# Block 1 of a three-block network: the delta rule and the gated branch written in turns of small steps

## The chip, the cores and the metric

One core of a Trainium2 chip runs the whole kernel as a single program. The metric is device time in microseconds (us), as the median of several runs. Engines are named as in the profile: PE is TensorE's matmuls and PEld its weight loads, DVE is VectorE, ACT is ScalarE, POOL is GpSimd, and SP is SyncE, which issues nearly all DMAs.

## The reference, cut to what matters

The reference has a first block and then a second one of depth two. Only the first block is touched. It works on 512 latent and 256 context positions of width 1024. From one normalized input and one projection it feeds three branches, whose results stand side by side, are multiplied by a gate and projected back:

```python
y_rc, y_rl = _rwkv_branch(u_c, u_l, ...)      # delta rule: 6 heads of 64, 2 directions
o_hc, o_hl = _hgrn_branch(fh_c, fh_l, ...)    # gated branch: 6 heads of 64, 2 directions
pool_l = _pool_branch(pv_l, True, pool_w[l], pool_scale[l])
mix_l = jnp.concatenate([pool_l, y_rl, o_hl], axis=-1) * jax.nn.silu(g_l)
new_x = _layer_norm(ALPHA * h_x + gt_l[:, None] * (mix_l @ w_out[l])) * ln_g[l] + ln_b[l]
```

The delta rule updates a matrix of 64x64 for each head and position, `S = S * w - (S kk) (kk a)^T + v k^T`, and reads it with `r`. The gated branch updates `S = exp(log f) * S + k i^T` and reads it with `q`. Both run over the context first and then, from that state, over the latent positions, once forwards and once backwards. They do not depend on each other.

## The kernel before

Both branches take two heads at a time, as 128 partitions, so there are three pairs `p`.

**The delta rule** is the generator `rwkv_pair(p)`. Its preparation makes the projections, the low-rank decay and rate (their bias is L690), and `rwkv_prep`, which builds the keys `BK` and the queries `AR` for both directions. Then come three groups `g` (context, and two halves of the latent positions), each of four chunks of 64 positions, with both directions side by side. A group has a state-free part, `rwkv_pre`: the score products (L763), transposes, and the inverse of a triangular matrix for each chunk, on VectorE and TensorE in turns. Its four calls of `rwkv_chunk` pass the state `st` on: POOL scales it (`pe`, L922), TensorE multiplies, ScalarE copies (`xs`), TensorE multiplies by the inverse, ScalarE and VectorE write `uv`, TensorE multiplies, and VectorE writes the new state (`rS`, L945, once for each direction). Then `rwkv_out` reads the group and `gate` projects one block of the output gate. The last group is followed by the pair's `readout` (its last line is L665). It yields after the preparation and after the first and second group.

**The gated branch** is `hgrn_pair(p)`: the projections `q` and `i`, and for each direction `dd` the projection `z` and one `hgrn_unit`. I number these six units 0 to 5 (pair 0 has units 0 and 1). A unit prepares the cumulated logarithms `hg` (first line L1048) and keys `kd`, then passes six chunks of 128 positions: two of the context, which only update the state `hS` (L1130), and four latent ones, for which `hgrn_levels` builds seven levels of products and each head's scores are reduced (`hrd`, L1096), copied to `sct` by ScalarE and multiplied. Its pair ends with a normalization (L1011). It yields once for each unit. Its projections write the PSUM tile `mf`, those of the delta rule `mm`; both go through `dense` (L277), which splits each weight block into two parts on ScalarE (L263) and VectorE (L264).

**Order.** `block1` draws steps of both generators in a loop over `n`:

```python
next(rw)
for n in range(6):
    for _ in range(2 - n % 2):
        next(rw, None)
    next(hg)
    ...                      # modulation: self.ada(...), and for n == 0 the pool branch
```

So an even `n` writes two groups of the delta rule and then a unit; an odd `n` writes the third group, the readout and the next pair's preparation, and then a unit. Behind each follows a modulation product (`ada`, matmuls L318 on weights that SP loads). The order in which a program is written is a rank for the library that lays out each engine's queue: an instruction whose inputs are ready goes by rank, and one that ranks later may stand ahead of one that is not ready. Each engine then works its queue in order, and waits for other engines through semaphores that the library places. Most tiles have one buffer, so that a unit's `z` or `hg` is not written before the unit ahead has read it. Behind the loop, `gated` multiplies the branches by the gate, and the next stage normalizes the context and projects with `w_out`.

Of the kernel before, what the change touches and what calls it, by code (L numbers as in the profile page):

```python
# [197 lines left out]
class B:  # L198
# [228 lines left out]
    def block1(self):  # L427
# [20 lines left out]
        with ExitStack() as ctx:  # L448
            ctx.enter_context(self.banks(mm=2, rsc=2, rch=1, mf=2, ma=1))
            ctx.enter_context(self.stream("f", 2, 1))  # L450
            ctx.enter_context(self.stream("a", 3, 1))
            self.scr = ctx.enter_context(tc.tile_pool(name="scr", bufs=1, space=bass.MemoryType.DRAM))
            self.f1 = ctx.enter_context(tc.tile_pool(name="f1", bufs=1))
            self.f2 = ctx.enter_context(tc.tile_pool(name="f2", bufs=2))
            self.con1 = self.f1.tile([128, CONST.shape[1] - NCON], F32, name="con1")
            nc.sync.dma_start(self.con1, d["const"][:, NCON:])
            self.ymix = self.scr.tile([128, 8, NL], F32, name="ymix")
            self.ygate = self.scr.tile([128, 8, NL], F32, name="ygate")
            self.ar = [[self.f1.tile([128, 4, 2, 2 if g else 1, 64], F32, name=f"AR{g}{dd}") for dd in range(2)] for g in range(3)]
            self.tt = self.f1.tile([128, 8, 2, 64], F32, name="rtt")  # L460
            for a in (*chain(*self.ar), self.tt):
                nc.gpsimd.memset(a, 0.0)
            self.sct = [self.f1.tile([128, 2, 128], F32, name=f"sct{a}") for a in range(2)]
            for x in self.sct:
                nc.gpsimd.memset(x, 0.0)
            self.rwkv_lora()
            self.hgrn_lb()
            self.last = {}
            rw = chain.from_iterable(self.rwkv_pair(p) for p in range(3))
            hg = chain.from_iterable(self.hgrn_pair(p) for p in range(3))  # L470
            next(rw)
            for n in range(6):
                for _ in range(2 - n % 2):
                    next(rw, None)
                next(hg)
                if n == 0:
                    self.ada(s, 0, d["mod_w"], 1, 2, mod[:, 16:24], self.V("mod_b", 16, 8), "a")
                    self.pool_branch()
                l, g = divmod(n, 3)
                self.ada(s, 2, d["ada_w"][l], g, 4, self.m2[l][:, 16 * g:16 * g + 16],  # L480
                         self.V("ada_b_2", 48 * l + 16 * g, 16), "a")
            hh, hl = self.htiles()

            def gated(j, y=None):
                a = y or self.f1.tile([128, NL], F32, tag=("tw", "ta")[j % 2], name="ga")
                b = self.f1.tile([128, NL], F32, tag=("G", "km")[j % 2], name="gb")
                if y is None:
                    nc.sync.dma_start(a, self.ymix[:, j])
                nc.sync.dma_start(b, self.ygate[:, j])
                nc.gpsimd.tensor_tensor(b, a, b, op=ALU.mult)  # L490
                self.split(hh[:, j, 256:], hl[:, j, 256:], b)

            for j in (0, 1, 2, 3, 5, 6):
                gated(j)
            for _ in chain(rw, hg):
                pass
            for j in (4, 7):
                gated(j, self.last[j])
# [116 lines left out]
    def rwkv_pair(self, p):  # L615
# [25 lines left out]
        for g in range(3):  # L641
            pre = self.rwkv_pre(g, bk, v)
            sts = []
            for i in range(4):
                sts.append(st)
                st = self.rwkv_chunk(g, i, ec[:, :, 4 * g + i], pre, st)
            if g:
                self.rwkv_out(g, sts, pre, y)
            if 3 * p + g < 8:
                self.gate(3 * p + g)  # L650
            if g < 2:
                yield
# [330 lines left out]
    def hgrn_pair(self, p):  # L983
        nc = self.nc
        f1, f2 = self.f1, self.f2
        q = f1.tile([128, NL], F32, name="hq")
        o, = self.dense(self.d["w_in"], 13 + p, self.hh, self.hl, (LAT,), st="f")
        nc.scalar.copy(q, o)
        it = f1.tile([128, 6, 128], F32, name="hit")
        ft = f1.tile([128, NT], F32, tag="htmp", name="hif")  # L990
        for (c0, cn), o in zip((LAT, CTX), self.dense(self.d["w_in"], 16 + p, self.hh, self.hl, (LAT, CTX), st="f")):
            nc.scalar.copy(ft[:, c0:c0 + cn], o[:, :cn])
        for c0, n in ((2, 4), (0, 2)):
            tp = self.psum("mf", (128, 4, 128))
            for j in range(n):
                nc.tensor.transpose(tp[:, j], ft[:, (c0 + j) * 128:(c0 + j + 1) * 128], self.C("ident"))
            nc.scalar.copy(it[:, c0:c0 + n], tp[:, :n])
        oa = f1.tile([128, NL], F32, name="hoa")
        for dd in range(2):
            z = f1.tile([128, NT], F32, name="hz")  # L1000
            for (c0, cn), o in zip((LAT, CTX), self.dense(self.d["w_in"], 19 + 3 * dd + p, self.hh, self.hl, (LAT, CTX), st="f")):
                nc.scalar.copy(z[:, c0:c0 + cn], o[:, :cn])
            self.hgrn_unit(p, dd, q, it, z, oa)
            yield
        sq = f1.tile([128, NT], F32, tag="htmp", name="osq")
        nc.gpsimd.tensor_tensor(sq[:, :NL], oa, oa, op=ALU.mult)
        va = self.psum("mf")
        nc.tensor.matmul(va, self.C("bones"), sq[:, :NL], start=True, stop=True)
        rs = f1.tile([128, NT], F32, tag="hg", name="ors")
        self.rsqrt_bc(rs[:, :NL], [(rs[:, :NL], va)], 1.0 / 64, 1)  # L1010
        nc.vector.scalar_tensor_tensor(oa, oa, self.V("hgrn_norm_g", p), rs[:, :NL], op0=ALU.mult, op1=ALU.mult)  # L1011
        self.last[5 + p] = oa
        if p < 2:
            nc.sync.dma_start(self.ymix[:, 5 + p], oa)
# [27 lines left out]
    def hgrn_unit(self, p, dd, q, it, z, oa):  # L1042
# [19 lines left out]
        for c in range(6):  # L1062
            nc.scalar.activation(kd[:, c], g[:, c], AF.Exp, scale=-1.0, bias=g[:, c, end:end + 1])
        nc.vector.tensor_tensor(kd, kd, k, op=ALU.mult)
        s = f2.tile([128, 128], F32, name="hS")
        nc.gpsimd.memset(s, 0.0)
        order = (0, 1, 2, 3, 4, 5) if dd == 0 else (1, 0, 5, 4, 3, 2)
        for n, c in enumerate(order):
# [49 lines left out]
            if n < 5:  # L1118
# [9 lines left out]
                for h in range(2):  # L1128
                    H = slice(64 * h, 64 * h + 64)
                    nc.vector.scalar_tensor_tensor(s2[H, H], s[H, H], ge[H, c:c + 1], tp[H, 1, 0:64], op0=ALU.mult, op1=ALU.add)  # L1130
                s = s2


    def block2(self):
# [646 lines left out]
```

## Time and profile before

| | us |
|---|---|
| median of 3 runs | 2727.29 (2724.37 to 2738.44) |
| profiled execution | 2736.78 |
| its span, first to last instruction | 2735.0 |
| PE busy in the span | 2523.7 (92%) |
| DVE / ACT / POOL busy | 1621.3 / 1276.9 / 319.3 |
| block 1's two branches | about 90 to 850 of the span |

The profile is one execution. "Busy" of PE counts matmuls that overlap and whose ends are modelled. PEclk is the clock granted to TensorE, as a share of 2.4 GHz; it has two levels, 1.0 and 0.5, so that a value between is a mean over a stretch. A row of a source line gives how often its instruction ran in a stretch, its duration, and when the first and the last of them started.

### The profile page before, as it was taken

The page shows a single profiled execution, that of the slowest core. Times are in us where ns is not written, and L with a number is a line of the kernel's source. Part 1 is how long each engine was busy: PE and PEld are TensorE (multiplying, and loading weights), DVE is VectorE, ACT ScalarE, POOL GpSimd, SP SyncE. Part 2 cuts the span into 40 slices and gives each one's busy share as a digit, 9 for nine tenths or more (in the row PEclk, how much of TensorE's full clock was granted, in tenths as well). Part 3 has the DMA queues.
Part 4 walks back from the last instruction along what each step waited for, and adds up shares of the span by engine and source line. Part 5 has one row for each costly group of instructions (what it writes and reads, how often), then busy time and mean ns, then how long its engine had stood idle before and what let it go on. Part 6 is the DMA issues. An engine that isn't in the chain of part 4 may idle for free.

```text
span 2735.0 us, 53289 instructions
## 1 busy us (share of the span) xinstructions
PE 2523.7 (92%) x21320; PEld 1990.5 (73%) x21320; DVE 1621.3 (59%) x3815; ACT 1276.9 (47%) x2840; POOL 319.3 (12%) x432
## 2 busy tenths in 40 slices
PE   7989979979877989989899999999998999999998
PEld 3655646545546777777677888888886888888888
DVE  4566574576565656777856443344463767664665
ACT  3454454545455656556434332233344555542444
POOL 0121121122112000111110110011000000010010
PEclk9999989989887999999989999999998999999999
DMA  6233432434334211111231112212231102233325
GB/s 206 77 94 118 139 98 92 125 100 134 93 104 146 72 39 32 36 41 37 65 105 47 62 63 64 63 63 66 80 105 44 32 27 95 78 100 93 100 89 157
DMA packets 159016, 231.10 MB, mean 84 GB/s; under 512 B 12976, under 2 KB 90032, under 8 KB 158768
## 3 DMA queue, kind: packets, MB, share of 16 engines
q1 hardware_dynamic: 158768, 227.70, 26.7%
q8 instruction: 167, 2.74, 0.4%
q14 instruction: 81, 0.66, 0.1%
HBM read 217.95 MB, written 9.70 MB: 83 GB/s over the span
## 4 chain that ended last, share of the span: by engine, by line
PE 47%; DVE 2%; ACT 2%; issue 1%; POOL 1%; DMA 0%; POOLq 0%; SPq 0%; DVEq 0%; ACTq 0%
PE mm L277 39%; PE ms L1735 2%; PE mt L1754 1%; PE mv L351 1%; PE mt L1748 1%; PE mm L1685 1%; PE mf L277 0%; DVE hl L423 0%; DVE ht L421 0%; POOL qr L1669 0%; ACT hh L422 0%; DMA raw<-mla_w_out 0%; ACT whi L263 0%; ACT qrh L1705 0%; PE mm L1665 0%
## 5 line engine op out<-in xcount | busy, mean ns | idle before, releaser
L264 DVE TENSOR_TENSOR wlo<-raw,whi 128x512 fp32r<-128x512 f32 (+3 forms) x560 | 391.3, 701 | 395.1 <-ACT whi L263 236.6
L263 ACT CAST whi<-raw 128x512 fp32r<-128x512 f32 (+3 forms) x560 | 331.9, 594 | 462.8 <-PE mm L277 398.9
L277 PE MATMUL mm<-hh,whi 128*128 128x512 f32 (+1 forms) x1960 | 483.8, 360 | 28.0 <-ACT hh L422 13.6
L277 PE MATMUL mm<-hl,whi 128*128 128x512 f32 (+1 forms) x1960 | 457.3, 350 | 0.0
L277 PE MATMUL mm<-hh,wlo 128*128 128x512 f32 (+1 forms) x1960 | 455.3, 350 | 0.4 <-DVE wlo L264 0.4
L277 PEld LDWEIGHTS mm<-hh,whi 128*128 128x128 f32 x1960 | 332.4, 192 | 89.7 <-ACT hh L422 21.0
L277 PEld LDWEIGHTS mm<-hl,whi 128*128 128x128 f32 x1960 | 329.7, 193 | 46.8 <-issue 3.6
L277 PEld LDWEIGHTS mm<-hh,wlo 128*128 128x128 f32 x1960 | 328.9, 193 | 45.0 <-issue 2.0
L1233 POOL TENSOR_TENSOR fc<-fc,fc 128x768 f32<-128x768 f32 (+1 forms) x44 | 69.2, 1573 | 867.9 <-DVE fc L585 625.8
L277 PE MATMUL mm<-fh,whi 128*128 128x256 f32 (+1 forms) x616 | 136.3, 340 | 1.0 <-ACT fh L398 1.0
L583 DVE SCALAR_TENSOR_TENSOR fc<-mm,vec,fc 128x511 f32<-128x511 f32 (+1 forms) x132 | 86.8, 658 | 80.7 <-ACT fc L582 80.7
L277 PE MATMUL mm<-fl,whi 128*128 128x256 f32 (+1 forms) x616 | 130.5, 330 | 0.0
L277 PE MATMUL mm<-fh,wlo 128*128 128x256 f32 (+1 forms) x616 | 129.3, 328 | 0.0
L582 ACT ACTIVATE fc<-mm,vec 128x512 f32<-128x512 f32 (+1 forms) x132 | 81.4, 617 | 97.2 <-PE mm L277 97.2
L277 PEld LDWEIGHTS mm<-fh,whi 128*128 128x128 f32 x616 | 99.8, 190 | 15.8 <-issue 3.4
L318 PE MATMUL ma<-raw,cvs 128*32 128x256 f32 x832 | 95.6, 427 | 15.3 <-DMA raw<-ada_w 10.6
L277 PE MATMUL mf<-hh,whi 128*128 128x512 f32 (+1 forms) x360 | 103.6, 387 | 6.0 <-ACT whi L263 3.4
L277 PEld LDWEIGHTS mm<-fl,whi 128*128 128x128 f32 x616 | 99.0, 190 | 11.3 <-issue 0.5
L1197 DVE SCALAR_TENSOR_TENSOR xr<-mm,m,xr 128x512 f32<-128x512 f32 (+1 forms) x112 | 66.5, 597 | 67.0 <-PE mm L277 66.8
L277 PEld LDWEIGHTS mm<-fh,wlo 128*128 128x128 f32 x616 | 98.6, 190 | 10.4
L351 PE MATMUL mv<-sq,con 128*128 128x256 f32 (+1 forms) x240 | 84.3, 452 | 12.4 <-ACT sq L355 12.0
L277 PE MATMUL mf<-hl,whi 128*128 128x512 f32 (+1 forms) x360 | 95.4, 367 | 0.0
(545 smaller groups left out, 4383.6 us busy)
## 6 DMA issues: line engine op xcount, KB each, us to landing
raw<-ada_w SPq DMA_DIRECT2D x96, 512.0 KB, 4.6
raw<-ffn_up SPq DMA_DIRECT2D x176, 256.0 KB, 2.8
raw<-ffn_down SPq DMA_DIRECT2D x96, 256.0 KB, 2.7
raw<-w_in SPq DMA_DIRECT2D x66, 256.0 KB, 2.9
raw<-ab_w_in SPq DMA_DIRECT2D x50, 256.0 KB, 2.6
raw<-ffn_down SPq DMA_DIRECT2D x48, 192.0 KB, 2.4
raw<-mod_w SPq DMA_DIRECT2D x16, 512.0 KB, 7.6
raw<-w_out SPq DMA_DIRECT2D x32, 256.0 KB, 2.9
```

Source lines behind the costliest of these rows:

```text
L263: nc.scalar.copy(hi[:, :nk], raw[:, :nk])
L264: nc.vector.tensor_tensor(lo[:, :nk], raw[:, :nk], hi[:, :nk].bitcast(F32), op=ALU.subtract)
L277: nc.tensor.matmul(o, a[:, k], b[:, k0 + k, t:e], start=(k0 == 0 and j == 0 and k == 0), stop=(k0 + n == nk and j == 2 and k == n - 1))
L318: nc.tensor.matmul(acc[32 * b:32 * b + 32, c:c + 256], s[:, k, :], t[:, b], start=(k == 0), stop=(k == 7))
L351: self.nc.tensor.matmul(v[:, :x.shape[1]], self.C("ones"), x, start=(k == 0), stop=(k == 7))
L582: nc.scalar.activation(out[:, c0:c0 + cn], o[:, :cn], AF.Copy, scale=w[1])
L583: nc.vector.scalar_tensor_tensor(out[:, c0 + 1:c0 + cn], o[:, :cn - 1], w[0], out[:, c0 + 1:c0 + cn], op0=ALU.mult, op1=ALU.add)
L1197: nc.vector.scalar_tensor_tensor(x, o[:, :cn], gcol(m, 0 if c0 else 1), x, op0=ALU.mult, op1=ALU.add)
L1233: nc.gpsimd.tensor_tensor(g, g, u, op=ALU.mult)
L1685: nc.tensor.matmul(o[:, e], a[:, k, T], b[:, k], start=(i == 0), stop=(i == 5))
L1735: nc.tensor.matmul(o[:, at:at + cn], a, b, start=(j == 0), stop=(j == 4))
L1748: nc.tensor.transpose(tp[:, j], p[:, (c0 + j) * 128:(c0 + j + 1) * 128], self.C("ident"))
```

## The change

No instruction is added or left out. Both generators get more places to yield, and the loop takes turns between them.

```diff
             next(rw)
             for n in range(6):
-                for _ in range(2 - n % 2):
-                    next(rw, None)
-                next(hg)
+                for i in range(4):
+                    next(hg)
+                    for _ in range(1 + (i == 1 and n % 2 == 0)):
+                        next(rw, None)
...
             for i in range(4):
+                if i % 2 == 0:
+                    yield
                 sts.append(st)
                 st = self.rwkv_chunk(g, i, ec[:, :, 4 * g + i], pre, st)
...
-            self.hgrn_unit(p, dd, q, it, z, oa)
+            yield from self.hgrn_unit(p, dd, q, it, z, oa)
             yield
...
         nc.vector.tensor_tensor(kd, kd, k, op=ALU.mult)
+        yield
         s = f2.tile([128, 128], F32, name="hS")
...
                 s = s2
+            if n in (1, 3):
+                yield
```

A step of the delta rule is now a state-free part, or the first two chunks of a group, or its last two with what follows them (output, gate, and after the third group the readout and the next preparation): nine steps for each pair. A step of the gated branch is the projections and the preparation of a unit, or its two context chunks, or two latent chunks with their levels: four steps for each unit. In each turn the gated step is written first. An even `n` writes: unit's preparation, state-free part 0; context chunks, four chunks of group 0 with its gate block; latent chunks, state-free part 1; latent chunks, two chunks of group 1. An odd `n` writes: preparation of the next unit, two chunks of group 1; context chunks, state-free part 2; latent chunks, two chunks of group 2; latent chunks, two chunks of group 2 with the readout and the next pair's preparation. The modulation products keep their places at the end of each `n`.

## Rows read from the trace of the kernel before

**Rows 1.** The profile page: the span of the profiled execution.

```profile
span 2735.0 us, 53289 instructions
```

**Rows 2.** Busy us (xcount) of PE, PEld, DVE, ACT, POOL by stretch; PEclk; DMA share, GB/s.

```profile
90.00:850.00 760.00, 653.29 (x9728) 420.75 (x9726) 465.42 (x1326) 381.91 (x1149) 148.77 (x265) 0.88 0.34 108
798.00:850.00 52.00, 27.57 (x528) 15.16 (x526) 31.92 (x89) 27.96 (x111) 15.11 (x18) 0.57 0.35 116
850.00:2735.00 1885.00, 1802.02 (x11259) 1529.43 (x11258) 1114.68 (x2412) 861.83 (x1636) 162.41 (x148) 0.98 0.23 70
```

**Rows 3.** Timeline of TensorE near 100 us: a projection of the gated branch (mf).

```profile
100.63 0.63 PE L277 MATMUL mf<-hh,wlo 128*128 128x512 f32 x2
```

**Rows 4.** New states of the delta rule by group (ns min/median/max, first and last start us).

```profile
L945 DVE SCALAR_TENSOR_TENSOR rS<-rch,rec,pe x8: 275/277/285, 176.3 to 190.9; 128x64 f32<-128x64 f32 x8
L945 DVE SCALAR_TENSOR_TENSOR rS<-rch,rec,pe x8: 275/278/284, 228.4 to 244.5; 128x64 f32<-128x64 f32 x8
L945 DVE SCALAR_TENSOR_TENSOR rS<-rch,rec,pe x8: 274/280/287, 423.0 to 437.0; 128x64 f32<-128x64 f32 x8
L945 DVE SCALAR_TENSOR_TENSOR rS<-rch,rec,pe x8: 252/276/284, 462.0 to 476.2; 128x64 f32<-128x64 f32 x8
L945 DVE SCALAR_TENSOR_TENSOR rS<-rch,rec,pe x8: 274/280/285, 537.4 to 551.1; 128x64 f32<-128x64 f32 x8
L945 DVE SCALAR_TENSOR_TENSOR rS<-rch,rec,pe x8: 275/276/285, 663.6 to 678.0; 128x64 f32<-128x64 f32 x8
L945 DVE SCALAR_TENSOR_TENSOR rS<-rch,rec,pe x8: 274/280/284, 706.3 to 721.2; 128x64 f32<-128x64 f32 x8
L945 DVE SCALAR_TENSOR_TENSOR rS<-rch,rec,pe x8: 274/280/284, 783.0 to 798.2; 128x64 f32<-128x64 f32 x8
```

**Rows 5.** Gated units: start of unit 4, then the reductions of units 0 to 5.

```profile
L1048 ACT ACTIVATE hg<-hz x1: 843/843/843, 720.3 to 720.3; 128x768 f32<-128x768 f32 x1
L1096 DVE TENSOR_REDUCE hrd<-hmp x8: 468/478/489, 210.2 to 247.9; 128x32 f32<-128x192 f32 x8
L1096 DVE TENSOR_REDUCE hrd<-hmp x8: 474/479/512, 341.4 to 396.4; 128x32 f32<-128x192 f32 x8
L1096 DVE TENSOR_REDUCE hrd<-hmp x8: 461/475/498, 490.1 to 518.8; 128x32 f32<-128x192 f32 x8
L1096 DVE TENSOR_REDUCE hrd<-hmp x8: 478/482/494, 617.4 to 644.3; 128x32 f32<-128x192 f32 x8
L1096 DVE TENSOR_REDUCE hrd<-hmp x8: 432/478/486, 739.3 to 764.5; 128x32 f32<-128x192 f32 x8
L1096 DVE TENSOR_REDUCE hrd<-hmp x8: 472/477/484, 811.6 to 837.6; 128x32 f32<-128x192 f32 x8
```

**Rows 6.** Low-rank bias of the decay, first step of each preparation behind its projections.

```profile
L690 DVE TENSOR_SCALAR tw<-mm,vec x4: 475/610/751, 111.2 to 129.0; 128x512 f32<-128x512 f32 x2, 128x256 f32<-128x256 f32 x2
L690 DVE TENSOR_SCALAR tw<-mm,vec x4: 474/612/751, 338.3 to 355.5; 128x512 f32<-128x512 f32 x2, 128x256 f32<-128x256 f32 x2
L690 DVE TENSOR_SCALAR tw<-mm,vec x4: 472/610/750, 567.2 to 585.5; 128x512 f32<-128x512 f32 x2, 128x256 f32<-128x256 f32 x2
```

**Rows 7.** Busy time in two groups, with unit 0 and without, then beside unit 4.

```profile
228.00:245.00 17.00, 17.00 (x369) 10.68 (x371) 12.81 (x44) 7.78 (x32) 3.65 (x10) 1.00 0.38 106
462.00:476.00 14.00, 14.00 (x206) 9.48 (x205) 5.40 (x16) 6.00 (x13) 1.26 (x4) 1.00 0.37 117
721.00:783.00 62.00, 51.20 (x1052) 30.81 (x1050) 38.37 (x127) 34.97 (x137) 7.50 (x17) 0.86 0.39 121
```

**Rows 8.** Ends of both branches, next stage's first matmul, TensorE's largest wait (us, times, longest).

```profile
L665 DVE SCALAR_TENSOR_TENSOR ry<-ry,vec,rpb x3: 743/746/752, 313.2 to 807.3; 128x512 f32<-128x512 f32 x3
L1011 DVE SCALAR_TENSOR_TENSOR hoa<-hoa,vec,ors x3: 750/752/1296, 403.4 to 845.0; 128x512 f32<-128x512 f32 x3
849.06 1.22 PE L351 MATMUL mv<-sq,con 128*128 128x256 f32 x2 [5.54 <-ACT sq L355]
PE rsc L763 <- DVE BK L727: 18.3, 4, 7.7
```

## The prediction

> **What bounds the kernel now.** I read the table of stretches first. Block 1's stretch, from 90 to 850 us, takes 760 us, and TensorE is busy for 653.3 of them; behind 850 us it is busy for 1802.0 of 1885.0, or 95.6% [rows 2]. So only the 760 us have slack that another order of the program could use: 106.7 us of TensorE's idle time, and a granted clock of 0.88 against 0.98 behind it. The last 52 us hold 24.4 us of that idle time, at a clock of 0.57. I read the page's chain of waits next; it does not reach back into this stretch, so what sets the length has to be read from when each part's steps begin and end.
>
> Two dependent chains run here. The delta rule's state is updated 36 times, in nine groups of four chunks; the end of each group and the start of the next show how long the part between them took [rows 4]. The gated branch is six units; each one's reductions show where it ran [rows 5]. The projections and the modulation products fill TensorE between them. The last state of the delta rule stands at 798.2 us, while the last gated unit reduces from 811.6 to 837.6 [rows 4, 5]: the last unit begins late, and its end is what the next stage waits for.
>
> That is readable from the program: of two things that are ready for an engine, the one written earlier goes first, but a later one starts when the earlier is not ready. A projection of the gated branch, written behind two groups of chunks, runs at 100.6 us, ahead of the first pair's low-rank part at 111.2 [rows 3, 6]. So the text's order is a rank and no fixed sequence. Before, units 0 and 5 rank behind the delta rule's work beside them, while units 2 and 4 rank ahead of the state-free part of the pair's third group.
>
> **The change, part by part.** No instruction is added or removed. 27 steps of the delta rule and 24 of the gated branch now alternate, a gated step ranking ahead of the delta step behind it. All their instructions move in rank: the projections' matmuls with weight loads on SP, the splits on ScalarE and VectorE, the small products and clearings on POOL. I price it by what one gated unit costs the delta rule's path.
>
> *What the units cost now.* A state-free part without a gated unit takes 437.0 to 462.0 and 678.0 to 706.3, a mean of 26.7 us; an undisturbed group, over the six rows of that kind, 14.3 us from its first state to its last [rows 4].
> - Unit 0 ranks behind: the part beside it takes 190.9 to 228.4, 10.8 us more, and the group from 228.4 to 244.5, 1.8 us more. Cost 12.6 us.
> - Unit 1, beside a preparation: from the first low-rank bias to the first state 338.3 to 423.0 is 84.7 us, against 111.2 to 176.3, 65.1 us, for the first pair [rows 4, 6]. Cost 19.6 us. Unit 3 likewise: 567.2 to 663.6, 96.4 us. Cost 31.3 us.
> - Units 2 and 4 rank ahead: 476.2 to 537.4 and 721.2 to 783.0, so 34.5 and 35.1 us more than 26.7.
> - Unit 5 runs alone: from the last state to the next stage's first matmul at 849.1 is 50.9 us [rows 4, 8]. If the delta rule ended last, what would stand there is its readout, to 808.1, and about 4 us from the last normalization to that matmul (845.0 to 849.1), together 13.9 us [rows 8]. Cost 37.0 us.
>
> The sum is 170 us, so if a unit costs c in the new order, the change is 6c - 170. Taking each unit's cost from unlike neighbours is rough, above all for units 1 and 3, whose neighbours also hold a modulation product.
>
> *What a unit costs in the new order.* Unit 4 lasts 45 us, from 720.3 to 765 [rows 5]. Its last two steps, which carry the levels and most of its time, now stand beside chunk steps at three of their four places in a pair of heads, one of them with the next preparation behind it, and beside a state-free part at one; its first two stand beside either at two places each. I take half of its time, 22.5 us, beside each.
> - Beside a state-free part, ranking ahead: 35/45 of its time by units 2 and 4, 17.5 us.
> - Beside a group of chunks, ranking ahead: no row shows it. The low end is the one group that had a unit beside it, 1.8 us (the unit ranked behind); below nothing is excluded, since the delta rule's instructions are the same and none of them is issued earlier than its inputs. The high end is the rate beside the state-free part, 35/45 of 15 us, or 12 us a group. I take 5 us, nearer the group's own row, because in a group the engines stand emptier: VectorE is busy for 5.4 of 14 us and ScalarE for 6.0 [rows 7]. For 1.5 groups that is 7.5 us.
>
> So c is 25 us (20.2 to 35), and the change 6 x 25 - 170 = -20 us.
>
> *What must give way.* The groups are already full on TensorE, 14.0 of 14 us, and stay full beside a unit, 17.0 of 17 [rows 7]: dense products fill them. What gated matmuls displace there has to run beside the state-free parts and preparations, which are rid of gated work; I count that at nothing. If that cover is gone the clock falls, as it did to 0.86 beside unit 4 [rows 7]; this is a mechanism of the second rival.
>
> *Queues.* Weight loads of the gated branch move ahead on SP of the delta rule's; the DMA engines are busy for 0.34 of the stretch [rows 2], so I price it at nothing, and one held load would cost the projection behind it only. On POOL the state's scaling at the start of each chunk stands behind the gated clearings; TensorE stands in order too: it waited 18.3 us in four waits for the preparation's keys while other work stood behind [rows 8]. A gated matmul ahead of a chunk's matmul, waiting for its copies on ScalarE, holds that chunk up: this is inside the 5 us.
>
> The Trainium skill, in Perfetto Trace Analysis, section Optimization Strategy, says that where the most-contended engine changes over time, interleaving the regimes can help; by that rule taken alone the sum would be the first rival's. The unit beside a group in rows 4 agrees with it, the units beside state-free parts do not. Against the change speaks TensorE: Matmul & The Clock Gate, section HAM oscillation: dense products should run without breaks, or the engine's clock falls back; by that rule the result is nearer the second rival, and the clock of 0.86 beside unit 4 against 1.00 in the groups agrees.
>
> **The rivals.**
> 1. Larger gain. Chunk groups absorb gated steps at 1.8 us each whatever the rank: c = 1.5 x 1.8 + 17.5 = 20.2, and the change -49 us, 2678. For it: the group beside unit 0. Against: that unit ranked behind; and 653 us of TensorE in 711 would need 92% busy, where it is now 86%.
> 2. Slower, by gated work ahead in every step. Each step of the delta rule stands behind gated copies and reductions and costs what units 2 and 4 do, c = 35: 6 x 35 - 170 = +40 us, 2767. It decides from c = 28.3 on, where the sum is zero, and shows from 30.6. For it: both units that ranked ahead cost 35. Against: they stood beside a part that has its own long chain on VectorE, and a chunk group has not.
> 3. Nothing measurable. The order is a rank only, the engines already take what is ready, and what the tail gives back is spent earlier: c from 26 to 30.6, 2727 within 13. For it: the projection at 100.6 us shows how far work already moves by itself, and the tail's 37 us are about one unit's cost. That the change does not do what it says is this case too.
>
> **How the numbers follow.** The profiled execution took 2736.8 us, 1.8 us more than its span [rows 1], and lies 9.5 us above the median of 2727.3. The sum gives 2736.8 - 20 = 2717 for a profile, and 2707 for the median. Chances: the forecast, c from 22 to 26, 0.38; larger gain, 0.16; nothing measurable, 0.25; slower, 0.21. About 0.5%, 14 us, is what a measurement of this kernel can tell from no change, so faster 0.54, same 0.25, slower 0.21. The forecast's own range is 2689 to 2713. The range for 8 in 10 runs from below the first rival to halfway into the second: 2672 to 2750.
>
> **What would show it.** If it is right, the last gated reduction comes before the last state of the delta rule, and from that state to the next stage's first matmul there are about 14 us instead of 50.9; the parts between groups that took 61 us take 45 to 50; groups take 17 to 20 us instead of 14.3; and nothing behind the next stage's first matmul changes its length. The step on the groups is wrong if they take over 25 us or under 16; the step on the tail is wrong if the gated branch still ends last. The whole is wrong if the preparations, which I left as they are, grow: their two stretches from bias to first state, 84.7 and 96.4 us, are where a gated first step with three projections now ranks next.

## The result, and the profile after

| | before | changed |
|---|---|---|
| median, us | 2728.74 | 2683.30 |
| lowest to highest | 2724.37 to 2738.44 | 2679.38 to 2689.75 |
| span of the profiled execution | 2735.0 | 2677.6 |

The ratio is 0.9838, with a 95% interval of 0.9816 to 0.9859: 44 us faster. The forecast was 20 us, so the sign was right and the size was less than half of what was measured. The first rival, 2678, came nearest. The two profiled executions lie further apart than the medians, 57.4 us by their spans: the one before ran 8 us above its median and the changed one 4 us below. Differences between these two profiles are too large by some 12 us in all.

The page of the changed kernel, its first lines (share of the span, count) and the clock by slices:

```profile
span 2677.6 us, 53279 instructions
PE 2498.0 (93%) x21320; PEld 1992.3 (74%) x21320; DVE 1615.7 (60%) x3815; ACT 1272.8 (48%) x2840; POOL 312.8 (12%) x432
PEclk9989998998979999999899999999998999999999
```

The table of stretches of the changed kernel, columns as in [rows 2]: both branches, what stands behind the last delta state, and the rest:

```profile
90.00:789.90 699.90, 619.89 (x9708) 415.65 (x9706) 459.60 (x1318) 374.98 (x1143) 141.33 (x264) 0.92 0.37 117
778.50:789.90 11.40, 3.22 (x5) 0.82 (x5) 3.39 (x7) 2.33 (x5) 3.34 (x4) 0.64 0.28 92
789.90:2677.60 1887.70, 1805.69 (x11260) 1532.93 (x11260) 1115.21 (x2416) 862.71 (x1638) 163.27 (x149) 0.97 0.23 70
```

The rest kept its length (1887.7 us, against 1885.9 from 849.1 on before; the profiles of all other runs have 1880 to 1890), so the gain is all in the stretch of the two branches: 759.1 us before, 699.9 now. TensorE's busy time there fell from 652.4 to 619.9 with the same matmuls, and its idle time from 106.7 to 80.0; the mean clock rose from 0.88 to 0.92.

Nearly all of this lies where the granted clock stood at the lower of its two levels. Summed over those stretches of the two branches, before and then changed (the first number is their length, the next is TensorE's busy time):

```profile
sum 176.98, PE 131.80 PEld 74.50 DVE 114.27 ACT 87.32 POOL 31.68; mean PE 7.75 PEld 4.38 DVE 6.72 ACT 5.14 POOL 1.86
sum 117.39, PE 100.51 PEld 62.96 DVE 67.33 ACT 65.83 POOL 12.30; mean PE 7.18 PEld 4.50 DVE 4.81 ACT 4.70 POOL 0.88
```

The time at the lower level fell by 59.6 us and the time at the full level stayed, 582.1 and 582.5 us (in the second profile of the changed kernel, e0 below, 128.1 at the lower level and 582.1 at the full). TensorE's idle time at the lower level fell from 45.2 to 16.9 us, and at the full level it did not fall. This says where the time went and not why: the order e3 below spends 178.8 us at the lower level and is still faster than the kernel before.

The source rows of the changed kernel, new states of the delta rule in five of its nine groups (the line is now L948), to be held against [rows 4]:

```profile
L948 DVE SCALAR_TENSOR_TENSOR rS<-rch,rec,pe x8: 272/278/284, 240.7 to 263.0; 128x64 f32<-128x64 f32 x8
...
L948 DVE SCALAR_TENSOR_TENSOR rS<-rch,rec,pe x8: 266/273/285, 479.3 to 495.4; 128x64 f32<-128x64 f32 x8
...
L948 DVE SCALAR_TENSOR_TENSOR rS<-rch,rec,pe x8: 273/276/285, 536.1 to 550.2; 128x64 f32<-128x64 f32 x8
...
L948 DVE SCALAR_TENSOR_TENSOR rS<-rch,rec,pe x8: 267/272/283, 709.4 to 725.4; 128x64 f32<-128x64 f32 x8
...
L948 DVE SCALAR_TENSOR_TENSOR rS<-rch,rec,pe x8: 273/280/284, 764.3 to 778.5; 128x64 f32<-128x64 f32 x8
```

The last unit's reductions, the last of [rows 5], and then the timeline of TensorE at the next stage's first matmul, the third of [rows 8]:

```profile
L1100 DVE TENSOR_REDUCE hrd<-hmp x8: 435/476/484, 731.1 to 767.8; 128x32 f32<-128x192 f32 x8
```

```profile
789.88 1.22 PE L351 MATMUL mv<-sq,con 128*128 128x256 f32 x2 [5.39 <-ACT sq L355]
```

The last reduction, at 767.8, is now ahead of the last delta state, at 778.5, and the next stage begins 11.4 us behind that state instead of 50.9. The delta rule's own end came 19.7 us earlier as well, although it now has unit 5 beside it: the parts before the third groups took 40.7 and 38.9 us (495.4 to 536.1, 725.4 to 764.3), where they had taken 61.2 and 61.8 [rows 4].

### The profile page after: what moved, and what is told of

The parts are those of the page before. It is cut to its first block, busy times and chain, and to the rows that moved or that the text cites. A ratio compares the mean times of both kernels' runs of the same rounds, so it can differ in the third digit from the quotient of the medians.

```text
span 2677.6 us, 53279 instructions
## 1 busy us (share of the span) xinstructions
PE 2498.0 (93%) x21320; PEld 1992.3 (74%) x21320; DVE 1615.7 (60%) x3815; ACT 1272.8 (48%) x2840; POOL 312.8 (12%) x432
## 4 chain that ended last, share of the span: by engine, by line
PE 73%; DVE 14%; ACT 7%; issue 3%; POOL 1%; DMA 1%; SPq 0%; POOLq 0%; DVEq 0%; ACTq 0%
PE mm L277 48%; PE mf L277 4%; PE mv L351 3%; PE ms L1741 2%; PE ma L318 1%; PE mt L1760 1%; PE rsc L766 1%; PE mt L1754 1%; DVE hl L423 1%; DVE wlo L264 1%; PE rsc L864 1%; PE mm L1691 1%; ACT sct L1103 1%; DVE ht L421 1%; PE mm L692 1%
## 5 line engine op out<-in xcount | busy, mean ns | idle before, releaser
L277 PEld LDWEIGHTS mm<-hh,whi 128*128 128x128 f32 x1960 | 331.6, 192 | 81.9 <-ACT hh L422 20.2
L277 PE MATMUL mf<-hh,wlo 128*128 128x512 f32 (+1 forms) x360 | 92.1, 372 | 0.5 <-DVE wlo L264 0.5
```

The costliest lines, as they stand in the source:

```text
L277: nc.tensor.matmul(o, a[:, k], b[:, k0 + k, t:e], start=(k0 == 0 and j == 0 and k == 0), stop=(k0 + n == nk and j == 2 and k == n - 1))
```

## The experiments

Two notes for all of them. Comparisons are ratios against the kernel before, run beside each on the same chip. A stretch of one profile can be off by some 10 us: the changed kernel's two branches ended at 789.9 in one profile and at 800.2 in another, of nearly the same span (2677.6 and 2680.0).

**The yardstick** (e0). The changed kernel again, unedited.

> The changed kernel once more, on the chip of the other three, as their yardstick. Both theories: 2683 us, ratio to the kernel before 0.982 to 0.986.

2682.2 us, ratio 0.9837 (0.9818 to 0.9855). As expected.

**Rank alone** (e1). Large steps as before, the gated unit written first.

```diff
-                for _ in range(2 - n % 2):
-                    next(rw, None)
                 next(hg)
+                for _ in range(2 - n % 2):
+                    next(rw, None)
```

> The old large steps (two groups, or one group with readout and preparation, against a whole gated unit), only with the gated unit written first. Theory A (rank: the gain is the gated branch no longer ending last; small steps add nothing): the tail behind the last delta state is about 11 us instead of 50.9, the parts between groups change little, 2680 to 2700 us. Theory B (place: a gated two-chunk step costs almost nothing beside a chunk group and much beside a state-free part, so small steps are needed): whole units ranking ahead of state-free parts cost about 35 us each as units 2 and 4 did before, what the tail gives is spent there, 2715 to 2750 us, with parts of 45 to 65 us between groups.

2722.5 us, ratio 0.9981 (0.9964 to 0.9998). The tail went, as in the change: 12.4 us from the last state, at 819.5, to the next stage. But the delta rule ended 21 us later than before. So the tail's 39.5 us are no gain by themselves; theory A falls.

**Small steps, delta rule first** (e2).

```diff
                 for i in range(4):
-                    next(hg)
                     for _ in range(1 + (i == 1 and n % 2 == 0)):
                         next(rw, None)
+                    next(hg)
```

> The new small steps, but in each turn the delta rule's step is written before the gated one. Theory A (rank): one gated step of two latent chunks is left behind the last delta step, so about 20 us of the 39.5 us that the tail lost in the profiles come back, 2700 to 2710 us. Theory B (place): the steps stand beside each other as in the changed kernel, only the last gated step trails, and the delta rule's own path is up to 10 us shorter for ranking ahead, 2685 to 2700 us.

2691.9 us, ratio 0.9875 (0.9854 to 0.9895). About three quarters of the gain need no change of rank within a turn; they come with the small steps, and the rank adds about 10 us.

**Latent steps ahead of state-free parts** (e3).

```diff
                 for i in range(4):
                     next(hg)
-                    for _ in range(1 + (i == 1 and n % 2 == 0)):
+                    for _ in range(((0, 0, 3, 2), (1, 0, 2, 1))[n % 2][i]):
                         next(rw, None)
```

> The new small steps, gated first, but with the draws shifted: three of the four latent steps of a pair are now written directly ahead of a state-free part (even n: preparation, context chunks, latent chunks, then state-free part 0 and all of group 0, latent chunks, then state-free part 1 and two chunks; odd n: as in the change but state-free part 2 behind the latent chunks). Theory A (rank): the branches end as in the changed kernel, 2680 to 2692 us. Theory B (place): four more latent steps rank ahead of state-free parts, each some 10 to 15 us dearer there than beside chunks, 2715 to 2740 us, with the parts of 38 to 41 us between groups grown to 50 or more.

2713.0 us, ratio 0.9940 (0.9920 to 0.9960): 31 us dearer than the change, just under theory B's range and far above theory A's. Place matters. The next two ask whether its price is a constant.

**The other way** (e5). The draws are (0, 1, 3, 1) in an even `n`: all four latent steps of a pair stand beside chunks.

> The changed kernel with the first latent step of each even unit moved from ahead of state-free part 1 to ahead of group 0's chunks, so that all four latent steps of a pair are written beside chunk steps (even n draws 0, 1, 3, 1 steps of the delta rule behind the four gated ones). Theory B (place): e3 moved six latent steps from chunks to state-free parts for 31 us, 5 us each; three moved the other way give about 15 us: 2662 to 2672 us. Theory C (throughput) or a saturated group: no more to be had, 2680 to 2695 us.

2685.5 us, ratio 0.9846 (0.9809 to 0.9882): no further gain. A latent step ahead of state-free part 1 seems to cost no more than one beside chunks; but the same edit moves the unit's context chunks from beside group 0 to ahead of state-free part 0, so a gain and a loss may have cancelled.

**State-free part 0 ahead of the unit's preparation** (e7), with draws (0, 1, 2, 1) behind it.

> As the changed kernel, but in even n state-free part 0 is written ahead of the gated unit's preparation, and the latent chunks stand ahead of group 0's second half. e2, with the delta rule first everywhere, had 67 to 70 us from low-rank bias to first state against 89 to 93 in the changed kernel, and longer parts 1 and 2. Theory B (place): the first states come 20 us earlier in each pair, and the unit's preparation is paid beside the chunks instead, at a lower price: 2660 to 2675 us. Theory C (throughput): what is saved there is given back behind it, 2680 to 2692 us.

2694.6 us, ratio 0.9871 (0.9839 to 0.9902). The first states did come earlier (174.7 instead of 196.7), and all of it and more was given back: the nine groups, 138 us together in the changed kernel, took 187. That is theory C's outcome, and slightly worse.

**Single chunks** (e6). Both generators yield after each chunk (of the unit's, after each latent one).

> Still smaller steps: one chunk of the delta rule, and one latent chunk of the gated branch (its two context chunks stay together), gated first, 15 delta steps and 12 gated ones for a pair, with state-free parts 1 directly behind the second latent chunk. Theory B (place): neighbours are the same kinds as in the changed kernel, each piece half as long, so little changes: 2675 to 2690 us. Theory D (grain: the gain comes from how little of the other branch ranks ahead at any time): another 10 us or more, 2660 to 2675 us.

2689.6 us, ratio 0.9858 (0.9828 to 0.9888). Nothing more is gained by a finer grain; theory D falls.

**Gate blocks one group later** (e10).

```diff
-            if 3 * p + g < 8:
-                self.gate(3 * p + g)
+            if 3 * p + g > 0:
+                self.gate(3 * p + g - 1)
```

> The changed kernel with its eight gate blocks (dense products that nothing in this stage waits for) each one group later: none behind the first group, the last one behind the ninth group instead of the eighth. In the profile after, 740 to 780 us have few dense products, a clock of 0.5 to 0.7 and 12 us of idle time. Theory C with the clock (dense products are the filler, and where they lack TensorE idles and runs at the lower level): the end fills, 2670 to 2680 us. If filler is as much needed early (the clock was 0.54 from 170 to 180 us): no change, 2680 to 2688 us. If the gate's last block delays the multiplication by the gate: 2685 to 2695 us.

2693.3 us, ratio 0.9873 (0.9851 to 0.9894): about 10 us worse, a time of the third expectation. But the profile's tail is 12.4 us (11.4 and 12.4 in the two profiles of the changed kernel), so the gate's last block is not what cost it. Early filler being missed would fit; that was not followed further.

**Without the units** (e4 with the new steps, e8 with the old). Both kernels with the six calls of `hgrn_unit` replaced by a sum of the two `z`, so that the gated branch is left out but for its projections and its normalization.

```diff
-            yield from self.hgrn_unit(p, dd, q, it, z, oa)
+            if dd == 0:
+                nc.gpsimd.memset(oa, 0.0)
+            nc.gpsimd.tensor_tensor(oa, oa, z[:, 256:], op=ALU.add)
...
```

> The changed kernel without the six gated units: their projections, the pair's normalization and all steps stay, but the branch's output is the sum of the two z projections. It measures what six units cost together: c = (time with - time without) / 6, for the changed kernel (2682) and the one before (2728). Theory B (place; the path analysis of the traces gives about 21 us a unit in the changed kernel and 28 to 30 before): 2545 to 2565 us. Theory C (throughput: a unit costs in the changed kernel what its small matmuls take on TensorE, 97 us for all six in the profile after): 2575 to 2595 us.

> The kernel before (large steps, delta rule first) without the six gated units, as e4 is the changed kernel without them (e4: 2586). It says whether the steps matter at all without units, and what six units cost in the old order. If the change's whole gain lies in how the units stand among the rest: 2580 to 2592 us, so units cost about 141 us before and 97 after. If part of the gain is in the delta rule's own steps (finer ranks for the projections and modulation products among its parts): 2600 us or more.

With the new steps 2586.1 us, ratio 0.9479 (0.9450 to 0.9508); with the old ones 2575.8, ratio 0.9443 (0.9422 to 0.9464). In parts of the time before, the units cost 0.9837 - 0.9479, or 98 us, in the new order, and 1 - 0.9443, or 152 us, in the old one: 16 and 25 us a unit. By the intervals these sums are good to about 9 and 6 us. Theory C's number for the new order is met, and theory B's 21 us a unit, 126 for six, is not; the old steps came out 4 us under the first range. Without units the new steps are 10 us slower by the medians, which the overlapping intervals hardly tell from nothing. So the whole gain, and perhaps 10 us more, lies in what the units cost.

The busy time of both without units, old steps and then new (columns as in [rows 2]):

```profile
90.00:689.80 599.80, 527.51 (x6683) 343.73 (x6681) 316.10 (x850) 228.77 (x508) 132.51 (x215) 0.95 0.42 136
```

```profile
90.00:697.30 607.30, 530.74 (x6682) 352.44 (x6680) 315.23 (x847) 228.49 (x508) 126.25 (x212) 0.93 0.42 134
```

In the new order the units add 89 us to TensorE's busy time (530.7 to 619.9) and 3 us of idle time (76.6 to 80.0); in the second profile of the changed kernel, e0, it is 92 and 11 (622.6 and 87.7). In the old order they add 125 us (527.5 to 652.4) and 34 us of idle time (72.3 to 106.7). To VectorE's busy time they add 144 us in the new order and 149 in the old.

**Dearer products, by mistake** (e9 in the changed kernel, e11 in the one before). Each level of a head as one product of 128 columns of weights instead of four of 32, in both kernels. I had meant to make them cheaper. The scores are not the branch's.

```diff
-                        for i in range(4):
-                            T = slice(J + 32 * i, J + 32 * i + 32)
...
-                            nc.tensor.matmul(sc[32 * i:32 * i + 32, 32 * l:32 * l + 32], a, bq, start=True, stop=True)
+                        a = lv[H, l, J:J + 128] if l < 5 else k[H, c]
+                        bq = lv[H, l, J:J + 32] if l < 5 else q[H, 128 * j:128 * j + 32]
+                        nc.tensor.matmul(sc[:, 32 * l:32 * l + 32], a, bq, start=True, stop=True)
```

> The changed kernel with a quarter of the units' small score products: each level of a head is one product of 128 columns of weights instead of four of 32 (their results are not the scores). Everything else of a unit, on VectorE, ScalarE and POOL, stays. 2304 matmul records of 41 us busy become 576. Theory C (throughput: a unit costs TensorE's time for its products): 25 to 32 us less than the changed kernel's 2683, 2650 to 2660 us. Theory B (the path of dependent steps sets what a unit costs): the records are no long part of a unit's path, 2672 to 2684 us.

> The same edit in the kernel before. There units cost 141 us against 105 us of their matmuls' busy time, so part of their cost is waiting and a halved clock. Theory C: the products' own time goes, 25 to 32 us, and since more idle time makes the halved clock more frequent a part is lost again: 2698 to 2708 us. Theory B: 2715 to 2728 us.

2726.6 us (ratio 1.0000, 0.9989 to 1.0011) with the new steps, and 2783.6 (1.0210, 1.0186 to 1.0234) with the old: 44 and 57 us *more* than the kernels they were made from. The groups of lines of the two branches' stretch show why, first in the changed kernel, then in this one (count, busy us, mean ns of one):

```profile
L1088 PE MATMUL mf<-hlv 64*32 64x32 f32 x1920 | 38.0, 209 | 9.9 <-issue 4.6 <-DVE hlv L1042 3.9 <-DVE hS L1134 1.0
L1088 PE MATMUL mf<-hq,hz 64*32 64x32 f32 x384 | 13.8, 207 | 0.0
```

```profile
L1086 PE MATMUL mf<-hlv 64*128 64x32 f32 x480 | 71.8, 313 | 2.9 <-DVE hlv L1042 2.0 <-DVE hS L1132 0.5 <-DVE hoa L1119 0.3
L1086 PE MATMUL mf<-hq,hz 64*128 64x32 f32 x96 | 18.7, 314 | 0.0
```

A quarter of the records keeps TensorE busy for longer: 90.5 us against 51.8, added over both rows. So the expected saving was wrong, and both times lie outside all ranges given. Seen from the other side, VectorE, ScalarE and POOL do what they did, TensorE has some 39 us more in the units, and the kernel takes 44 us more. That fits theory C. It does not rule out theory B, because the products also stand in each unit's own path and grew there from 209 to 313 ns a record. Nor is the 39 us the whole: over the two branches TensorE is busy for 681.5 us here, 62 more than in the changed kernel, and idle for 67.0, 13 less. And the old order, whose units cost more than their products take, paid 57 us for the same edit.

**Filling the tail** (e12 and e13). The kernel before, with useless products in unit 5 only; `r` is 1, and then 2.

```diff
                     sc = self.psum("mf")
+                    if p == 2 and dd == 1:
+                        for _ in range(r):
+                            nc.tensor.matmul(sc, self.C("ident"), self.xw[:, :512], start=True, stop=True)
...
                 op = self.psum("mf")
+                if p == 2 and dd == 1:
+                    for _ in range(r):
+                        nc.tensor.matmul(op, self.C("ident"), self.xw[:, :512], start=True, stop=True)
```

> The kernel before with 12 useless dense products (128x512, about 0.85 us each at the full clock) in unit 5, which runs alone at the end: one ahead of each head's score products and of each chunk's output product, in the same PSUM tile, overwritten afterwards. TensorE gets about 10 us more to do in the last 50.9 us, where it idles for 24 us at the half clock. If the halved clock is a cause of the tail's length (products took 238 ns there against 193 ns beside other work): the granted clock of the tail rises and the tail gets no longer or shorter, 44 to 51 us, 2720 to 2727 us. If it is only a mark of an idle engine: the fill lies in the unit's path and the tail grows by 3 to 10 us, 2730 to 2738 us.

> As e12 with 24 such products, some 20 us of fill in 24 us of idle time. If the clock is a cause: the tail's clock is near 1.0, and the tail stays within 3 us of 50.9, 2725 to 2731 us. If it is a mark only: the tail grows by 10 to 20 us, 2738 to 2748 us.

2728.5 us (ratio 1.0003, 0.9990 to 1.0015) and 2736.2 (1.0030, 1.0019 to 1.0041). Both times fall between the two ranges expected: one fill cannot be told from none, two cost 8 us. The lengths of the tails say more. These are the stretches from the last delta state to the next stage, with one fill and then with two (columns as in [rows 2]):

```profile
793.90:849.10 55.20, 39.12 (x548) 17.49 (x540) 32.68 (x88) 27.24 (x108) 14.23 (x18) 0.72 0.31 100
```

```profile
795.10:855.30 60.20, 44.76 (x571) 20.02 (x571) 32.65 (x88) 27.19 (x108) 16.06 (x19) 0.88 0.29 93
```

The fill raised the mean clock of the tail from 0.57 to 0.72 and 0.88, and the median record of the unit's score products fell from 238 to 211 and 193 ns. Yet the tail grew from 50.9 to 55.2 and 60.2 us, in one profile each. TensorE had 12.6 and 18.2 us more to do; two thirds and half of that went into idle time, the rest lengthened the unit's path, by 4.3 and 9.3 us, and the faster products did not give it back. In the tail the lower clock goes with an engine that waits. How much of the 32 us by which TensorE's busy time fell in the whole stretch is a cause of the gain, this does not settle: it was tried where a unit runs alone, and not where dense products run at the lower level. An estimate bounds it: the fill's dense products took 592 ns a record at the full level and 1061 at the lower, 1.8 times as long; if all that TensorE did at the lower level (131.8 us before, 100.5 after) had been stretched as much, the clock would account for 0.44 of the 31.3 us between them, or some 14 of the 32 us.

**One cut alone** (e14). Units in four steps, gated first, but a group of the delta rule in one step again.

```diff
-                if i % 2 == 0:
-                    yield
...
                 for i in range(4):
                     next(hg)
-                    for _ in range(1 + (i == 1 and n % 2 == 0)):
+                    if i == 0 or (i == 2 and n % 2 == 0):
                         next(rw, None)
```

> One part of the change alone: the gated units are cut into their four steps, gated first, but a group of the delta rule stays one step (even n: preparation, group 0; context and latent chunks, group 1; latent chunks; odd n: preparation, group 2 with readout and preparation; then the three other steps). e1, with whole units, was at 2722, the change at 2682. Theory C (throughput: what a unit costs above its TensorE time comes from stretches in which only dependent work of both branches is left): half of the cuts give part of the gain, 2695 to 2710 us. If cutting the delta rule's groups between state-free part and chunks is what matters: 2715 to 2727 us. If cutting the units is: 2680 to 2692 us.

2740.9 us, ratio 1.0044 (1.0026 to 1.0061): slower than before, and outside all three ranges. An odd `n` writes the next preparation behind the unit's first step here, and the unit's other three steps behind the preparation. Two stretches beside preparations, in the kernel before, in this one and in the changed one (columns as in [rows 2]):

```profile
345.00:385.00 40.00, 26.32 (x308) 14.62 (x309) 34.86 (x79) 17.41 (x52) 12.03 (x17) 0.66 0.34 106
578.00:612.00 34.00, 19.32 (x112) 10.50 (x110) 31.05 (x58) 15.60 (x31) 13.53 (x14) 0.65 0.43 138
```

```profile
350.00:390.00 40.00, 21.76 (x280) 12.14 (x279) 36.37 (x90) 19.32 (x54) 13.99 (x20) 0.70 0.38 117
610.00:640.00 30.00, 17.25 (x187) 9.78 (x188) 25.10 (x63) 10.74 (x27) 11.11 (x13) 0.67 0.46 138
```

```profile
350.00:390.00 40.00, 36.20 (x196) 24.48 (x197) 32.66 (x64) 18.85 (x29) 12.49 (x22) 0.91 0.52 158
580.00:620.00 40.00, 33.03 (x187) 21.00 (x187) 31.50 (x61) 17.79 (x28) 13.47 (x26) 0.89 0.47 153
```

Behind each stretch's length stands TensorE's busy time first and VectorE's third. Where a unit's preparation or levels meet a delta rule's preparation, VectorE is busy for 84 to 91% and TensorE for 54 to 66%, at a mean clock of 0.65 to 0.70. In the changed kernel the unit has finished by then, and the preparation stands beside the next unit's dense projections: VectorE is at 79 to 82%, and TensorE is busy for 83 to 91%. TensorE's wait for the keys that VectorE writes in a preparation, 18.3 us before [rows 8], shows what that is worth over both branches, in the changed kernel and then in this one:

```profile
PE rsc L766 <- DVE BK L730: 8.0, 4, 2.5
PE rsc L764 <- DVE BK L728: 20.3, 5, 8.7
```

So VectorE is the bound in these places, but they are a part of the matter: 12 of the 30 us by which this kernel's idle time (110.2 us) is above the changed one's. What the other 18 are was not followed. The other cut alone, groups of the delta rule in three steps and units whole, was not run, so what either cut is worth by itself stays open.

## Why the prediction was right in sign and wrong in size

The nine groups' first and last states cut the stretch of 759.1 us into pieces. Summed for four kernels, from 90 us to the next stage's first matmul:

| us | before | its steps without units | difference | changed | its steps without units | difference |
|---|---|---|---|---|---|---|
| to the first state | 86.3 | 84.1 | 2.2 | 106.7 | 92.1 | 14.6 |
| nine groups | 131.0 | 124.5 | 6.5 | 138.1 | 126.9 | 11.2 |
| six parts between groups of a pair | 260.7 | 193.8 | 66.9 | 206.6 | 196.4 | 10.2 |
| two stretches from pair to pair | 230.2 | 170.5 | 59.7 | 237.1 | 179.5 | 57.6 |
| behind the last state | 50.9 | 26.9 | 24.0 | 11.4 | 12.4 | -1.0 |
| sum | 759.1 | 599.8 | 159.3 | 699.9 | 607.3 | 92.6 |

The differences, 159.3 and 92.6, are those of single profiles; the medians gave 152 and 98.

*What a unit costs in the new order* is the step that failed. I took c as 25 us, with 20.2 as the low end; the runs without units give 98/6, or 16. Both of its terms were too high. Beside the groups I took 5 us each, or 45 for nine; the table has 11.2, which is 1.2 a group and under my low end of 1.8. Beside the state-free parts I carried over the rate of units 2 and 4, 17.5 us a unit and 105 for six. Those parts stand at three places of a pair, and the first of them lies in the rows to the first state and from pair to pair; the three rows together have 82.4, with what the preparations paid in it. So this term was too high by less, but it was put in the wrong place: the six parts between groups, where the rate was read, grew by 10.2, and the two of 61 us took 40.7 and 38.9 instead of the 45 to 50 that I gave. That rate belonged to a whole unit with a modulation product and the next unit's start ranking ahead of one part; a step of two chunks ahead of it is another thing, and e1 and e14, where whole units or three steps in a row come together again, have most or all of the old length back (242 and 267 us for the six parts, against 261 before and 207 in the changed kernel).

*What the units cost now* failed less. My sum was 170 us; the runs without units say 152. The tail was too dear by the same table: 24.0 us and not 37.0, since it holds 26.9 us even without units. Units 2 and 4 were priced against parts of 26.7 us; without units the parts before the third groups take 28 to 36. With 152 and 98 the same formula gives -54, and the 10 us that the new steps cost without units make it -44. That has to be so, since all come from the same four times; it shows the size of each term and tests nothing.

*The first rival* came within 5 us by luck. Its c of 20.2 is above the 16 measured, its 170 us above the 152, and it has nothing for the 10 us; the errors cancel. My argument against it, that 653 us of TensorE in 711 would need 92%, took TensorE's busy time as fixed. It fell to 620, which is 89% of 700.

*What was left out.* The stretches from pair to pair cost as much with the change as before, 58 against 60 us. Before, I had priced units 1 and 3 there at 51 us; in the new order I had counted the preparations at nothing. They now hold other work: dense projections, where before the levels of a unit stood beside the preparation.

*The form of the sum.* Pricing a unit by how much one piece of the delta rule's path grows is the deeper fault. e2 and e7 shorten the stretches from pair to pair (187 and 196 us instead of 237) and lengthen groups and parts by more: work moves from piece to piece. What adds up is the whole stretch, as TensorE's busy and idle time: 652.4 + 106.7 before, 619.9 + 80.0 after. In the new order the units cost 98 us, about what their matmuls take on TensorE (101 us busy in the profile after); in the old one they cost 152 against 105, some 50 us above it. That TensorE's time is what a unit costs now is the reading that fits best; two numbers that agree do not show it, and no run took TensorE's time alone away.

*What held.* The branches' ends exchanged as forecast, with 11.4 us behind the last state against the 14 expected; nothing behind moved; six groups stayed at about 14 us and two took 16, under the 17 to 20 that I gave; one took 22.3, with unit 1's cumulated logarithms, keys and dense projections beside it, and why it alone is not shown; the preparations did not grow by much (84.7 and 96.4 us from bias to first state became 90.2 and 88.0). The Trainium skill, in Perfetto Trace Analysis, section Optimization Strategy, says that interleaving stretches with different most-contended engines may help; this case agrees, by 44 us. The Trainium skill, in TensorE: Matmul & The Clock Gate, section HAM oscillation, tells of a kernel in which each wait between short runs of products brought the clock down again. More of that did not come here: the stretch's mean clock rose from 0.88 to 0.92.

None of the orders tried is faster than the changed kernel; e5 and e6, at ratios of 0.9846 and 0.9858, cannot be told from it.

## What to carry to other kernels

Before pricing two interleaved branches by how much one delays the other, take one of them out and run: the difference in time, set beside its own time on the busiest engine, suggests how much an order could still save. Here it was 152 us against 105 before and 98 against 101 after, and no order tried was faster than the second. Write steps so that the work that is heavy on one engine stands beside work that is heavy on another, and check pairs, not averages: where two parts that both want VectorE met, TensorE was busy for 54 to 66%, in a stretch where it is busy for 86% on average. Letting the shorter branch go first is worth little by itself; what it saves at the end it can spend in the middle.

## What the runs showed of the hardware

The 960 score products of 64x32 weights in the first five levels, four to a level, each on its own 32 output partitions, leave two records each in the trace. These 1920 records of 209 ns overlap so far that they keep TensorE busy for 38.0 us, 158 ns for four products. One product with 64x128 weights in place of four takes 299 ns of it (240 products, 480 records, in 71.8 us), nearly twice what the four take together. Busy times of matmuls rest on modelled ends; the 44 us by which the kernel became slower do not.

Useless dense products in a waiting engine raised the mean granted clock of the tail (0.57 to 0.88) and shortened the unit's score products (238 to 193 ns a record), and the path that they stood in still grew, from 50.9 to 60.2 us.
